# A 32-byte pad at the right edge of SBUF in an encoder-block kernel

## The chip, the cores and the metric

The kernel runs on one core of a Trainium2 chip. The metric is the device time of one execution in microseconds, as a median of runs; before the change it is 1386.01 us (three runs, 1385.64 to 1386.95).

## The reference

One encoder block with 1024 positions and a model width of 1024, all in float32. Cut to what matters:

```python
proj = x @ w_in[l]                      # q, k, v of attention; q, k, v, gates of the GLA; merge gates
...
y_attn = ...                            # three groups of dilated window attention, mixed
y_gla  = ...                            # gated linear attention in both directions, normed and gated
merged = (jax.nn.sigmoid(gate_a) * (y_attn @ w_attn_branch[l])
          + jax.nn.sigmoid(gate_g) * (y_gla @ w_gla_branch[l]))
x = _layernorm(ALPHA * x + merged @ w_out[l], ln1_g[l], ln1_b[l])
ff = jnp.square(jax.nn.relu(x @ w_ff1[l] + b_ff1[l])) @ w_ff2[l] + b_ff2[l]   # 1024 -> 4096 -> 1024
x = _layernorm(ALPHA * x + ff, ln2_g[l], ln2_b[l])
```

## The kernel before

**Products in three passes.** Each float32 operand is split into a high part that TensorE takes at full speed (float32r) and a low part, the rest; ScalarE writes the high one, VectorE the low one. The helper `mm3` then issues three matmuls for each slice of 128 of the sum, on its lines 101 to 103, so almost every matmul of the profile has one of these lines:

```python
for i, (lh, ll, rh, rl) in enumerate(pairs):
    T.matmul(ps, lh, rh, ...)           # line 101: stationary, moving
    T.matmul(ps, lh, rl, ...)           # line 102
    T.matmul(ps, ll, rh, ...)           # line 103
```

The first SBUF operand is stationary (128x128, loaded into the array ahead of the matmul; the profile shows the load as engine PEld), the second moves (128x512). In the profile both stand behind the arrow, as in `ps<-B,fwhi`.

**The stages, in order of time.** Input projections; attention and linear attention, woven together; then from about 597 us the branch stage (`merge_a`, `merge_g`), the output projection `wout`, the first layer norm (`ln1`, and transposes of its result in `x1t`), the first feed-forward product (`pair1`), the second (`group`), and the last layer norm (`fin`). A scheduler sets the order of instructions from the order of the code.

The two feed-forward products and most projections use Strassen-Winograd: seven products of half-size blocks instead of eight. Their operands are sides: tiles of the shape [128, 2, 4, 512] with the high and the low part. In the first product the activations are the moving sides B11, B21, B22, T1, T2, T3, T4, and the weights of a pair of column blocks are split into the stationary sides `fwhi`, `fwlo`, `fraw`, `wc`, two buffers deep ahead. A pair has seven steps of 12 matmuls, one for each of these moving sides; there are 16 pairs. Pairs 0 and 1 take two of their seven weight blocks from the tile `early`. In the second product 28 times (4 groups of 7) a left block (`hp`, the hidden layer read back from DRAM) and a right block (`wa`, `wb`, weights) are split into two of six tiles that are used in turn, in this order, two for a product of 48 matmuls:

```python
sides = [X[nm] for nm in ("B11", "B21", "T3", "T1", "T4", "B22")]
```

**The output projection.** `wout` runs over 8 row tiles for each half of the columns. Stationary is the merged activation `mg` (`mg00`, `mg01` for row tiles 0 to 3, `mg10`, `mg11` for 4 to 7), moving the weights, which for the first half are `wo`, for the second `whi` and `wlo`:

```python
merge_streams([lambda t=t, ks=ks: wout(t, 0, w, ps[t], ks) for ks in (range(0, 4), range(4, 8)) for t in range(8)],
              park(0) + park(1))
```

So the first half is four blocks of 48 matmuls: row tiles 0 to 3, 4 to 7, then both again.

**Where tiles lie.** A pool opens at the left end of SBUF's free space, or with `side="right"` at the right end, growing towards the left. The left pools start behind small constants at an address of 0 modulo 64 and hold tiles of multiples of 64 bytes where it matters here. The right end of what the pools may use is 229344, which is 32 modulo 64; so all big tiles of right pools lie at 32 modulo 64. From the branch stage on these are on the right: pool `actb` (line 1007: `mg00`, `mg01`, later `early`, `B22`, `T4`), `woa` and `wob` (`wo`), `c0`, `xraw`, `res` and `pf` (`hp`, `wa`). All else is on the left.

Of the kernel before, what the change touches and what calls it, by code (L numbers as in the profile page):

```python
# [7 lines left out]
F32 = mybir.dt.float32  # L8
# [63 lines left out]
def build(tc, io):  # L72
    nc = tc.nc
    V, G, A, T, SP = nc.vector, nc.gpsimd, nc.scalar, nc.tensor, nc.sync
    P = Pools(tc)
# [108 lines left out]
    for k in range(KT):  # L184
        n = {0: 1, 1: 1, 2: 2, 4: 2, 6: 2}.get(k)
# [759 lines left out]
    for i in range(8):  # L945

        n = n0 - 18 + i * 3 // 2
# [54 lines left out]
    def load_gate(wi, hf):  # L1002
        g = gtp.tile([128, 512], F32, tag="gate", bufs=9, name="gate")
        SP.dma_start(g, spill[wi, :, hf * 512:hf * 512 + 512])
        return g

    bp = P.open("actb", bufs=2, side="right")
    mg = [[bp.tile([128, 2, 4, 512], F32R, tag="actb", name=f"mg0{i}") for i in range(2)],
          [xp.tile([128, 2, 4, 512], F32R, tag="act", name=f"mg1{i}") for i in range(2)]]
# [149 lines left out]
    c0 = c0p.tile([128, 5, 512], F32, name="c0")  # L1159
# [308 lines left out]
    def run(steps, ahead):  # L1468
        for prep, _ in steps[:ahead]:
            prep()  # L1470
        for i, (_, do) in enumerate(steps):
            if i + ahead < len(steps):
                steps[i + ahead][0]()
            for f in do:
                f()
# [229 lines left out]
        (SP if t == 2 else A).dma_start(io["out"][t * 128:t * 128 + 128, lo:hi], h)  # L1705

    run([st for g in range(NG) for st in group(g)], 2)
    for n in ("r2", "acc2", "pf", "c0", "actb"):
        P.close(n)
    for n in ("ps8", "dram", "act", "const"):  # L1710
        P.close(n)
# [74 lines left out]
def make(arrays):  # L1786
    import concourse.bacc as _bacc
    nc = _bacc.Bacc("TRN2", target_bir_lowering=False, num_devices=1, dynamic_dma_scratch_size=1024)
    io = {}
    for n, a in arrays.items():  # L1790
        io[n] = nc.dram_tensor(f"in_{n}", a.shape, mybir.dt.from_np(a.dtype), kind="ExternalInput").ap()
    io["out"] = nc.dram_tensor("out_0", (S, D), F32, kind="ExternalOutput").ap()
    with tile.TileContext(nc, schedule_with_timeline_sim=True) as tc:
        build(tc, io)
    return nc
# [8 lines left out]
```

## Time and profile before

| | |
|---|---|
| timed runs | 1386.01 us median (1385.64 to 1386.95) |
| profiled execution | span 1382.5 us from the first to the last instruction; the page gives no other time for it |
| TensorE (PE) busy | 1373.9 us, 99% |
| weight loads (PEld) | 1152.6 us, 83%, beside the matmuls |
| VectorE (DVE) busy | 1010.4 us, 73% |
| ScalarE (ACT) busy | 630.6 us, 46% |
| GpSimd (POOL) busy | 99.3 us, 7% |
| HBM | 172 GB/s over the span |

How to read it: rows of the timeline give a start, a duration, engine, line, operation and tiles. A matmul's duration there (0.39 us) is that of a pipeline, and matmuls overlap; the rate is read from the starts of successive ones. Rows of windows give for a stretch its length, then for PE, PEld, DVE, ACT and POOL the busy time and the count of instructions, then TensorE's granted clock (1.00 is full), the share of the DMA engines that is busy, and GB/s. Rows of waits read "engine, what waited <- what ended the wait: us in total, times, longest".

### The profile page before, as it was taken

To read this page: it belongs to the slowest core of one execution; us is meant where nothing else is said; L and a number is where in the kernel's file an instruction comes from. 1 tells how busy PE (TensorE), PEld (TensorE's weight loads), DVE (VectorE), ACT (ScalarE), POOL (GpSimd) and SP (SyncE) were. 2 spreads that over 40 slices of the span, in tenths; PEclk is the share of its full clock that TensorE was granted. 3 is DMA by queue.
4 is the path that set the end of the run, shared out by engine and by line. 5 is a ranking of instruction groups with operands and counts; after the bars stand their busy time and mean duration, and the time that the engine had idled before them with its cause. 6 is when DMAs were issued, how large, how long until landed. Compare 5 with 4: busy or idle time off the path is not lost.

```text
span 1382.5 us, 19028 instructions
## 1 busy us (share of the span) xinstructions
PE 1373.9 (99%) x6837; PEld 1152.6 (83%) x6837; DVE 1010.4 (73%) x1748; ACT 630.6 (46%) x1207; POOL 99.3 (7%) x153
## 2 busy tenths in 40 slices
PE   9999999999999999999999999999999999999998
PEld 7989998888888888888888788888888888888886
DVE  6377768776665678567757777877767897786988
ACT  5356645334434344455316655555456433333333
POOL 0000100022322232000001000000000000000002
PEclk9999999999999999999999999999999999999999
DMA  7262326765554443465934465656654965445313
GB/s 256 62 204 74 120 72 219 205 198 156 172 163 136 133 148 125 153 226 190 342 121 177 168 233 191 215 204 213 224 200 150 373 210 167 152 130 161 105 31 122
DMA packets 105907, 238.57 MB, mean 173 GB/s; under 512 B 20101, under 2 KB 28805, under 8 KB 105812
## 3 DMA queue, kind: packets, MB, share of 16 engines
q1 hardware_dynamic: 99220, 218.47, 47.4%
q0 software_dynamic: 6304, 18.49, 4.4%
q8 instruction: 54, 0.88, 0.3%
q10 hardware_dynamic: 288, 0.39, 0.1%
q14 instruction: 41, 0.34, 0.1%
HBM read 160.67 MB, written 77.68 MB: 172 GB/s over the span
## 4 chain that ended last, share of the span: by engine, by line
PE 96%; DVE 2%; ACT 1%; issue 0%; DMA 0%; SPq 0%; ACTq 0%; DVEq 0%
PE ps L101 18%; PE ps L103 18%; PE ps L102 18%; PE mm L101 10%; PE mm L102 10%; PE mm L103 10%; PE avp L844 3%; PE sc L803 2%; PE tr L830 2%; PE ps L1192 0%; PE sc L406 0%; PE tr L376 0%; DVE L L341 0%; PE sc L101 0%; PE sc L103 0%; PE sc L102 0%
## 5 line engine op out<-in xcount | busy, mean ns | idle before, releaser
L1176 ACT CAST T<-hp 128x1024 fp32r<-128x1024 f32 x36 | 37.8, 1050 | 110.3 <-PE ps L102 70.6
L102 PE MATMUL mm<-wlo,x 128*128 128x272 f32 (+1 forms) x240 | 74.5, 310 | 0.7 <-DVE wlo L94 0.7
L101 PE MATMUL mm<-whi,x 128*128 128x272 f32 (+1 forms) x240 | 75.0, 313 | 0.0
L103 PE MATMUL mm<-whi,x 128*128 128x272 f32 (+1 forms) x240 | 74.7, 311 | 0.0
L814 ACT ACTIVATE e<-e,sm 128x256 f32<-128x256 f32 (+2 forms) x96 | 43.4, 453 | 51.7 <-DVE sm L809 51.7
L102 PE MATMUL ps<-B,B 128*128 128x512 f32 x160 | 62.4, 390 | 0.0
L103 PE MATMUL ps<-B,B 128*128 128x512 f32 x160 | 62.3, 389 | 0.0
L101 PE MATMUL ps<-B,B 128*128 128x512 f32 x160 | 61.0, 391 | 0.5 <-ACT B L1176 0.5
L103 PE MATMUL ps<-B,T 128*128 128x512 f32 x144 | 56.2, 390 | 0.0
L101 PE MATMUL ps<-B,T 128*128 128x512 f32 x144 | 56.2, 390 | 0.0
L103 PE MATMUL ps<-T,T 128*128 128x512 f32 x144 | 56.1, 390 | 0.0
L101 PE MATMUL ps<-T,T 128*128 128x512 f32 x144 | 56.0, 389 | 0.0
L102 PE MATMUL ps<-T,T 128*128 128x512 f32 x144 | 56.0, 389 | 0.0
L102 PE MATMUL ps<-B,T 128*128 128x512 f32 x144 | 56.0, 389 | 0.0
L1177 DVE TENSOR_TENSOR T<-hp,T 128x1024 fp32r<-128x1024 f32 x36 | 43.9, 1220 | 15.3 <-ACT T L1176 15.2
L1577 DVE TENSOR_TENSOR acc<-ps,acc 128x512 f32<-128x512 f32 x68 | 45.5, 684 | 12.9 <-PE ps L103 12.2
L642 DVE TENSOR_TENSOR cr<-cu,mm 128x512 f32<-128x512 f32 x44 | 35.1, 799 | 23.7 <-PE mm L103 23.5
L1682 POOL TENSOR_TENSOR mv<-mv,mhalf 128x1 f32<-128x1 f32 x8 | 7.1, 882 | 611.4 <-DVE mv L1681 609.9
L101 PE MATMUL mm<-x,pwlo 128*128 128x512 f32 x128 | 51.0, 398 | 0.0
L101 PE MATMUL ps<-T,fraw 128*128 128x512 f32 x128 | 50.0, 394 | 0.3 <-ACT T L1176 0.3
L102 PE MATMUL ps<-T,fraw 128*128 128x512 f32 x128 | 50.1, 392 | 0.0
L103 PE MATMUL ps<-T,fraw 128*128 128x512 f32 x128 | 50.1, 392 | 0.0
(497 smaller groups left out, 4227.3 us busy)
## 6 DMA issues: line engine op xcount, KB each, us to landing
hdr<-c SPq DMA_DIRECT2D x112, 256.0 KB, 2.3
hp<-hdr SPq DMA_DIRECT2D x56, 512.0 KB, 3.6
spill<-cr SPq DMA_DIRECT2D x64, 256.0 KB, 2.8
praw<-in_wfm SPq DMA_DIRECT2D x16, 512.0 KB, 5.0
pwhi<-in_wfm SPq DMA_DIRECT2D x16, 512.0 KB, 4.5
gate<-spill SPq DMA_DIRECT2D x32, 256.0 KB, 3.4
wa<-in_w SPq DMA_DIRECT2D x16, 512.0 KB, 4.7
wb<-in_w SPq DMA_DIRECT2D x16, 512.0 KB, 6.3
```

Source lines behind the costliest of these rows:

```text
L101: T.matmul(ps, lh, rh, start=first and i == 0, stop=False, skip_group_check=more)
L102: T.matmul(ps, lh, rl, start=False, stop=False, skip_group_check=more)
L103: issued["pe"] = T.matmul(ps, ll, rh, start=False, stop=last and i == n - 1, skip_group_check=more)
L642: issued["add"] = V.tensor_tensor(o, a, b, op=OP.add)
L803: mm = T.matmul(sps[i][:, pr, 0:w], q[ps_, pr], k[ps_, pr, 0:w], start=True, stop=True)
L814: issued["exp"] = A.activation(e, e, AF.Exp, bias=sm[:, h:h + 1], scale=-1.0, accum_out=sm[:, 4 + h:5 + h])
L830: T.transpose(tp[0:hi - lo, pr, j], b["e"][i][:, pr, lo:hi], ident)
L844: return T.matmul(av[:, h * 64:h * 64 + 64], b["et"][h % 2][p0:p0 + vv.shape[0], h // 2, j], vv[:, h * 64:h * 64 + 64], start=j == h == 0, ...
L1176: A.copy(o[:, 0], src)
L1177: V.tensor_tensor(o[:, 1], src, o[:, 0].bitcast(F32), op=OP.subtract)
L1577: V.tensor_tensor(m, p, m, op=OP.add)
L1682: G.tensor_tensor(mv[:, 3:4], mv[:, 2:3], mhalf[:, 0:1], op=OP.pow)
```

## The change

A pool `pad` with one tile of 8 float32 a partition, 32 bytes, is opened on the right ahead of the first right pool of the branch stage, and closed at the end. No instruction writes or reads it.

```diff
+    P.open("pad", side="right").tile([128, 8], F32, name="pad")
     bp = P.open("actb", bufs=2, side="right")
     mg = [[bp.tile([128, 2, 4, 512], F32R, tag="actb", name=f"mg0{i}") for i in range(2)],
           [xp.tile([128, 2, 4, 512], F32R, tag="act", name=f"mg1{i}") for i in range(2)]]
...
-    for n in ("r2", "acc2", "pf", "c0", "actb"):
+    for n in ("r2", "acc2", "pf", "c0", "actb", "pad"):
         P.close(n)
```

The addresses that the built programs give to the tiles (bytes within a partition; the rest modulo 64 in brackets):

| tiles | pool | before | after |
|---|---|---|---|
| mg00, early, T4 | actb, right | 196576 (32) | 196544 (0) |
| mg01, B22 | actb, right | 212960 (32) | 212928 (0) |
| wo, eight tiles | woa, wob, right | 163808 to 192480 (32) | 163776 to 192448 (0) |
| c0 | c0, right | 186336 (32) | 186304 (0) |
| xr0, xr1 | xraw, right | 153568, 169952 (32) | 153536, 169920 (0) |
| ga, bb, tb, four res | res, right | 165856 to 184288 (32) | 165824 to 184256 (0) |
| four hp, four wa | pf, right | 153568 to 182240 (32) | 153536 to 182208 (0) |
| mg10, T1 | act, left | 52160 (0) | the same |
| mg11, T3 | act, left | 19392 (0) | the same |
| B11, B21 | act, left | 3008, 35776 (0) | the same |
| T2 | x7, left | 112064 (0) | the same |
| fwhi, fwlo, fraw, whi, wlo | w, left | 68544 to 107712 (0) | the same |
| wc6 | f1, left | 132544 (0) | the same |
| px, x11 (input projections) | cx, act, left | 177600, 19392 (0) | the same |

In all, 31 tiles move by 32 bytes.

## The prediction

> **What bounds the kernel now.** I read the page from the top, then the waits of TensorE, then single stretches of the timeline. The page's head, its clock row and its chain:
>
> ```profile
> span 1382.5 us, 19028 instructions
> PE 1373.9 (99%) x6837; PEld 1152.6 (83%) x6837; DVE 1010.4 (73%) x1748; ACT 630.6 (46%) x1207; POOL 99.3 (7%) x153
> PEclk9999999999999999999999999999999999999999
> PE 96%; DVE 2%; ACT 1%; issue 0%; DMA 0%; SPq 0%; ACTq 0%; DVEq 0%
> ```
>
> The reader is to see that TensorE is busy 99% of the span, that 96% of the chain that ended last is TensorE, and that its clock is never throttled. What TensorE still waits for, in its four longest rows of the waits:
>
> ```profile
> PE zp L180 <- DVE mhalf L211: 1.2, 1, 1.2
> PE ps L1703 <- ACT dg L1702: 1.0, 1, 1.0
> PE mm L102 <- DVE wlo L94: 0.7, 2, 0.4
> PE mm L101 <- ACT x L148: 0.5, 1, 0.5
> ```
>
> That is 3.4 us of 1382.5, so no wait is worth removing; time can only come from the rate of the matmuls themselves. "A busy PE is not PE at its peak", so I looked at how fast equal matmuls follow each other. The output projection is made for this: four blocks of 48 matmuls of 128x512, alike but for where their operands lie. The stationary operand is mg, the moving one wo. Windows cut at the first matmul of each block, with the matmuls and weight loads on mg alone:
>
> ```profile
> core 0: us, PE busy (x) PEld busy (x) DVE busy (x) ACT busy (x), PEclk, DMA share, GB/s
> 661.59:672.50 10.91, 10.91 (x48) 9.01 (x48) 2.08 (x3) 1.79 (x3) 1.00 1.04 398
> 672.50:683.70 11.20, 11.20 (x50) 9.00 (x49) 0.00 (x0) 0.00 (x0) 1.00 0.79 263
> 683.70:694.58 10.88, 10.88 (x49) 9.01 (x48) 0.00 (x0) 0.00 (x0) 1.00 0.80 305
> 694.58:705.77 11.19, 11.19 (x49) 9.00 (x48) 0.00 (x0) 0.00 (x0) 1.00 0.46 180
> ```
>
> (Counts over 48 are neighbours that overlap the window's edge.) Blocks 1 and 3 read mg00 and mg01 from pools on the right, 2 and 4 read mg10 and mg11 from the pool act on the left; wo is on the right in all four. By the address table above, left tiles stand at 0 modulo 64 and right tiles at 32. So 1 and 3 pair 32 with 32: 10.91/48 = 227.3 ns and 10.88/48 = 226.7 ns a matmul. 2 and 4 pair 32 with 0: 11.20/48 = 233.3 and 11.19/48 = 233.1 ns. The DMA share falls through 1.04, 0.79, 0.80, 0.46 and does not follow the steps; the clock is 1.00 in all. The weight loads take 9.00/48 = 187.5 ns in fast and slow blocks alike: what slows is the stream of the moving operand, while the next weights are read beside it.
>
> Is it the address, or only that one tile is low in memory and the other high? The input projections have a pair that tells: stationary px at 177600, which is as high as wo, but in a left pool, and moving x at 19392. First matmul of a step of 12, and first of the next step:
>
> ```profile
> 245.74 0.39 PE L101 MATMUL mm<-x,px 128*128 128x512 f32 x1
> 248.46 0.39 PE L101 MATMUL mm<-x,pwlo 128*128 128x512 f32 x1
> ```
>
> 2.72 us for 12, which is 226.7 ns: far apart, both at 0 modulo 64, and fast. I take 226.7 ns as the rate without the conflict.
>
> **The change, part by part.** It adds no instruction and reorders none: each engine's instructions stand in the built program in the same order as before; only 31 tiles lie 32 bytes lower. All pairs that were 32 with 0 become 0 with 0, and 32 with 32 becomes 0 with 0 too. So the work is to count the matmuls that now pair 32 with 0, and to price one.
>
> They are 624. Output projection, first half (moving wo right, stationary mg10/mg11 left): 4 row tiles x 8 slices x 3 = 96. Second half (moving whi/wlo left, stationary mg00/mg01 right): 96. Early weights (stationary on the right, moving B11 and B21 on the left): 2 pairs x 2 steps x 12 = 48. First feed-forward product: in each of 16 pairs the steps with T4 and with B22 (moving right, stationary left), 32 x 12 = 384. In the second product the operands come from six sides, and the sides of the right pool, T4 and B22, are always used with each other: no mixed pair, except where a product of the one kind follows one of the other.
>
> The price in the first feed-forward product, step by step. The first row is T3 (left), the second and fourth T4 (right), the third and fifth B11 (left), all against left weights:
>
> ```profile
> 788.02:790.74 2.72, 2.72 (x13) 2.25 (x12) 2.49 (x4) 1.19 (x2) 0.00 (x0) 1.00 0.01 3
> 790.74:793.54 2.80, 2.80 (x13) 2.25 (x12) 2.76 (x5) 2.74 (x6) 0.00 (x0) 1.00 0.25 94
> 793.54:796.30 2.76, 2.76 (x13) 2.25 (x12) 2.76 (x6) 2.76 (x5) 0.00 (x0) 1.00 0.51 190
> 796.30:799.10 2.80, 2.80 (x13) 2.25 (x12) 2.80 (x6) 1.19 (x3) 0.00 (x0) 1.00 0.92 341
> 799.10:801.86 2.76, 2.76 (x13) 2.25 (x12) 2.76 (x6) 2.38 (x5) 0.00 (x0) 1.00 0.50 187
> ```
>
> A mixed step costs 0.08 us more than 2.72, and the clean step behind it still 0.04 more: the stream seems to need a few matmuls to settle. By these rows a mixed step is worth (11.12 - 4 x 2.72)/2 = 0.12 us. The longer stretches, which hold all such effects:
>
> ```profile
> 661.59:705.77 44.18, 44.18 (x193) 36.02 (x192) 31.06 (x43) 13.35 (x18) 0.00 (x0) 1.00 0.77 286
> 705.77:716.98 11.21, 11.21 (x50) 9.02 (x48) 4.45 (x8) 0.62 (x1) 0.57 (x1) 1.00 0.25 102
> 801.86:1060.17 258.31, 258.31 (x1130) 211.65 (x1128) 197.21 (x307) 136.60 (x218) 0.00 (x0) 1.00 0.60 203
> 1060.17:1076.68 16.51, 16.51 (x73) 13.51 (x72) 10.94 (x15) 10.83 (x16) 0.00 (x0) 1.00 0.71 222
> 1076.68:1131.19 54.51, 54.51 (x241) 45.04 (x240) 50.45 (x55) 22.78 (x24) 0.00 (x0) 1.00 0.90 327
> ```
>
> With the weight loads as the count of matmuls and 226.7 ns (2.72/12) as the floor:
> - Output projection, first half: 44.18 - 192 x 0.22667 = 0.66 us.
> - Second half: 11.21 - 48 x 0.22667 = 0.33 us for 48, twice: 0.66 us.
> - First feed-forward product: 258.31 - 1128 x 0.22667 = 2.63 us, which holds 26 of the 32 mixed steps (0.10 each); 16.51 - 72 x 0.22667 = 0.19 us for two more; 0.10 each for the four of the pairs 0 and 1: 3.22 us.
> - Second product: 54.51 - 240 x 0.22667 = 0.11 us. It has 28 products of 48, 27 of them behind 1076.68: 1296/240 x 0.11 = 0.59 us if all of it is due to the switches between kinds of pairs, about 0.2 if each of some 24 switches costs one matmul its 6.7 ns. I take the middle, 0.4.
> - Early weights: the rows below.
>
> ```profile
> 759.85 0.40 PE L102 MATMUL ps<-B,early 128*128 128x512 f32 x1
> 761.48 0.39 PE L103 MATMUL ps<-B,early 128*128 128x512 f32 x1
> 761.91 0.59 ACT c L1319
> 762.50 1.65 ACT T L1176 x4
> 764.68 2.80 ACT xr L1195 x8
> 768.62 1.24 PE ps L101 x4
> ```
>
> Seven matmuls in 1.63 us are 232.9 ns each, so 48 x 6.2 = 0.30 us. But from 761.91 to 768.62 the chain runs through ScalarE (the last four rows are of the chain), so the 24 matmuls beside it gain nothing: 0.15 us.
>
> Sum: 0.66 + 0.66 + 3.22 + 0.4 + 0.15 = 5.1 us, all on TensorE and nearly all on the chain. The weak term is the settling, since I know no cause for it. Without any of it, 624 less the 24 hidden matmuls by 6.2 ns give 3.7 us; with all of it 5.3.
>
> Other engines: I cost the 32 bytes at nothing there. VectorE's operations with two operands in SBUF, by where these lie (wb, T1 and T3 left; wa and hp right):
>
> ```profile
> L1554 DVE TENSOR_TENSOR wb<-wb,wb x8: 1212/1218/1222, 1087.1 to 1286.0; 128x1024 f32<-128x1024 f32 x8
> L1554 DVE TENSOR_TENSOR wb<-wb,wa x8: 1212/1216/1219, 1086.0 to 1284.3; 128x1024 f32<-128x1024 f32 x8
> L1554 DVE TENSOR_TENSOR wa<-wb,wa x8: 1214/1218/1220, 1083.7 to 1280.3; 128x1024 f32<-128x1024 f32 x8
> ```
>
> Medians of 1216 to 1218 ns for equal and for mixed addresses: no effect. If that cover fails, VectorE has room where it counts (197.21 of 258.31 us in the first feed-forward product).
>
> [...]
>
> **The rivals.**
> A, nothing changes. The slow pairs would then owe their 6 ns to something that goes with the sides, such as tag or distance, and keep it: 1386.0 us. Against it stands px, high and fast. For it: before has no left-right pair at equal addresses. [...]
> B, the gain in the first feed-forward product is taken back because ScalarE and VectorE can't prepare sides faster: 1386.0 - (5.1 - 3.2) = 1384.1 if all of it is. Against it: ScalarE waits there for TensorE to free its buffers,
>
> ```profile
> ACT fraw L1176 <- PE ps L102: 42.0, 23, 3.3
> ```
>
> so a faster TensorE frees them sooner. What would be late next is VectorE at 76%.
> C, slower: DMAs into the moved tiles land later. The page's issues:
>
> ```profile
> hp<-hdr SPq DMA_DIRECT2D x56, 512.0 KB, 3.6
> wa<-in_w SPq DMA_DIRECT2D x16, 512.0 KB, 4.7
> wb<-in_w SPq DMA_DIRECT2D x16, 512.0 KB, 6.3
> ```
>
> wa (right, 32) lands in 4.7 us and wb (left, 0), of the same size, in 6.3. If the address were the reason, wa at 0 would take 1.6 us more: 16 x 1.6 = 25.6 us of landing. It decides once over 5.1 us of that reaches TensorE, a fifth; with a half, 1386.0 - 5.1 + 12.8 = 1393.7. Against it: wb is issued right behind wa on the same queue, reason enough for 6.3, and the loads are issued two steps ahead, where a step of 48 lasts 10.9 us.
>
> **How the numbers follow.** The page gives no time for the profiled execution besides its span, 1382.5; the three timed runs have a median of 1386.01 (1385.64 to 1386.95), 3.5 above it. I take the gain off the median: 1386.0 - 5.1 = 1380.9 us, and 1377.4 for the span. Chances: the forecast 0.86, A 0.05, B 0.06, C 0.03. 0.2% (2.8 us, 1383.2) is about what a measurement of this kernel can tell from no change. The forecast and half of B lie beyond it: faster 0.89; A and the other half of B: same 0.08; C: slower 0.03. The range: gains of 3.7 to 5.3 us, 0.65 more on either side for how the runs before spread around 1386, and B's halfway house: 1379.9 to 1383.4.
>
> **What the profile after would show.** The windows of the output projection at 10.9 us for all four blocks, the five steps of the first feed-forward product at 2.72 each, and its 1128 matmuls in about 255.7 us instead of 258.3; weight loads still at 187.5 ns, VectorE's times unchanged. If blocks 2 and 4 keep 11.2, A is right; if they fall but the 1128 matmuls don't, B; if TensorE waits for hp or wa, C. If mixed steps fall to 2.72 and the steps behind them stay at 2.76, the settling was something else, and the gain is nearer 3.7.

## The result and the profile after

The changed kernel takes 1380.3 us (median of five runs, 1379.72 to 1383.76), where the one before takes 1386.0. The ratio of the times is 0.9961, with a 95% interval of 0.9949 to 0.9972: 5.4 us faster, 3.9 to 7.1 by the interval. The ratios here and below leave out two executions far off the rest, one of before at 2099.97 us and one of `both32` at 1515.93 us. The forecast was 1380.9.

The page of after, its head and its clock row:

```profile
span 1382.0 us, 19028 instructions
PE 1370.8 (99%) x6837; PEld 1153.0 (83%) x6837; DVE 1011.3 (73%) x1748; ACT 630.7 (46%) x1207; POOL 99.1 (7%) x153
PEclk9999999999999999999999999999999999999998
```

Its chain, and the three longest waits of TensorE:

```profile
PE 90%; DVE 3%; DMA 2%; issue 2%; ACT 2%; POOL 0%; SPq 0%; POOLq 0%; ACTq 0%; DVEq 0%
```

```profile
PE mm L101 <- DVE cu L642: 1.4, 1, 1.4
PE zp L180 <- DVE mhalf L211: 1.2, 1, 1.2
PE mm L101 <- ACT x L148: 1.0, 1, 1.0
```

TensorE still carries the chain and waits for little; that DMA stands in it with 2% is mostly due to loads in the input stage, such as `pwhi`, 5.08 us from 235.02 on. The instructions are as many as before, and TensorE is 3.1 us less busy in all. But the span is 1382.0 us, hardly below the 1382.5 of before, though the median fell by 5.7. The reader must look at where the stretch that the change touches begins and ends. The first matmul on `wo` and the last one of a product in three passes (below: the last matmul), in the timelines of before and of after:

```profile
661.59 0.39 PE L101 MATMUL ps<-wo,mg 128*128 128x512 f32 x1
1371.81 0.39 PE L103 MATMUL ps<-B,B 128*128 128x512 f32 x1
```

```profile
665.99 0.39 PE L101 MATMUL ps<-wo,mg 128*128 128x512 f32 x1
1370.81 0.39 PE L103 MATMUL ps<-B,B 128*128 128x512 f32 x1
```

From the one to the other it was 710.22 us and is now 704.82: 5.40 us less. Ahead of it, where no matmul reads a tile that has moved, this execution lost 4.40 us, all of it before the branch stage, whose first matmul on `ya` starts at 596.30 us in before and at 600.71 in after. Behind it 0.50 us were lost (10.69 us from the last of these matmuls to the end, now 11.19). It was the slowest timed run of after (1383.76 us); the other four have spans of 1377.9 to 1378.6. Such a difference in the start comes with any kernel here: the same first matmul on `wo` stands at 662.30, 662.62, 663.75 and 664.29 us in experiments below. So I compare kernels by their medians and by the distance between those two matmuls, which the start doesn't enter.

The four blocks of the output projection in after, by the same windows as before (matmuls and weight loads on `mg` alone; PE, PEld, DVE, ACT, clock, DMA share, GB/s):

```profile
665.99:676.87 10.88, 10.88 (x49) 9.01 (x48) 2.78 (x4) 2.46 (x4) 1.00 1.01 379
676.87:687.75 10.88, 10.88 (x50) 9.01 (x48) 0.00 (x0) 0.00 (x0) 1.00 0.75 281
687.75:698.63 10.88, 10.88 (x50) 9.01 (x48) 0.00 (x0) 0.00 (x0) 1.00 0.94 325
698.63:709.51 10.88, 10.88 (x50) 9.01 (x48) 0.00 (x0) 0.00 (x0) 1.00 0.41 157
```

All four last 10.88 us, which is 226.7 ns a matmul; the 11.20 and 11.19 of blocks 2 and 4 are gone, and the 10.91 of block 1 too. The weight loads took 9.00 to 9.01 us a block and take 9.01. The five steps of the first feed-forward product that stood at 2.72, 2.80, 2.76, 2.80 and 2.76 (these windows have POOL as well):

```profile
790.87:793.59 2.72, 2.72 (x13) 2.25 (x12) 2.49 (x4) 1.19 (x2) 0.00 (x0) 1.00 0.01 3
793.59:796.31 2.72, 2.72 (x13) 2.25 (x12) 2.68 (x5) 2.66 (x6) 0.00 (x0) 1.00 0.26 96
796.31:799.03 2.72, 2.72 (x13) 2.25 (x12) 2.72 (x5) 2.72 (x6) 0.00 (x0) 1.00 0.51 191
799.03:801.75 2.72, 2.72 (x13) 2.25 (x12) 2.72 (x6) 1.31 (x3) 0.00 (x0) 1.00 0.87 325
801.75:804.47 2.72, 2.72 (x13) 2.25 (x12) 2.72 (x5) 2.22 (x4) 0.00 (x0) 1.00 0.51 191
```

The mixed steps have lost their 0.08, and the clean steps behind them their 0.04. The longer stretches of after (second half of the output projection, its first 48 matmuls; from its last block to the third pair of the feed-forward product; then the stretches of the prediction):

```profile
709.51:720.39 10.88, 10.88 (x50) 9.01 (x48) 9.02 (x16) 1.86 (x3) 0.57 (x1) 1.00 0.48 195
758.29:804.47 46.18, 45.78 (x211) 37.63 (x210) 37.03 (x62) 32.36 (x68) 0.93 (x1) 1.00 0.55 207
804.47:1060.15 255.68, 255.68 (x1129) 211.72 (x1128) 197.63 (x308) 136.59 (x219) 0.00 (x0) 1.00 0.60 206
1060.15:1076.47 16.32, 16.32 (x73) 13.51 (x72) 10.87 (x15) 10.83 (x16) 0.00 (x0) 1.00 0.72 225
1076.47:1130.87 54.40, 54.40 (x241) 45.05 (x240) 50.33 (x55) 22.78 (x24) 0.00 (x0) 1.00 0.90 329
1349.27:1371.03 21.76, 21.76 (x97) 17.83 (x95) 20.81 (x51) 8.16 (x20) 4.58 (x5) 1.00 0.34 127
```

Two rows of before that the prediction doesn't show, the counterparts of the second and the last:

```profile
755.17:801.86 46.69, 46.42 (x211) 37.62 (x210) 37.27 (x63) 32.60 (x69) 0.93 (x1) 1.00 0.55 205
1350.02:1372.04 22.02, 22.02 (x97) 17.84 (x95) 20.84 (x51) 8.19 (x20) 4.59 (x5) 1.00 0.34 126
```

From these rows and from the ends of stretches in them, the whole of the 5.40 us is found again (the third row also holds two steps behind pairs 0 and 1):

| stretch | before | after | less | forecast |
|---|---|---|---|---|
| output projection, first half | 44.18 | 43.52 | 0.66 | 0.66 |
| second half, to the start of the next row | 49.40 | 48.78 | 0.62 | 0.66 |
| early weights, pairs 0 and 1 | 46.69 | 46.18 | 0.51 | 0.15 + 0.40 |
| 1128 matmuls of the first feed-forward product | 258.31 | 255.68 | 2.63 | 2.63 |
| its last 24, with the first 48 of the second product | 16.51 | 16.32 | 0.19 | 0.19 |
| the rest of the second product, to the last group's end piece | 273.34 | 272.80 | 0.54 | 0.4 in all |
| end piece, to the last matmul | 21.79 | 21.54 | 0.25 | |

VectorE's operations with two operands, the same three groups as before, which stood at 1218, 1216 and 1218 ns:

```profile
L1555 DVE TENSOR_TENSOR wb<-wb,wb x8: 1220/1224/1228, 1088.1 to 1285.4; 128x1024 f32<-128x1024 f32 x8
L1555 DVE TENSOR_TENSOR wb<-wb,wa x8: 1219/1221/1226, 1086.9 to 1283.7; 128x1024 f32<-128x1024 f32 x8
L1555 DVE TENSOR_TENSOR wa<-wb,wa x8: 1218/1220/1222, 1084.7 to 1279.7; 128x1024 f32<-128x1024 f32 x8
```

They are 2 to 6 ns longer, whether or not their operands changed their places against each other: nothing was won here, and nothing that matters lost.

### The profile page after: what moved, and what is told of

It is laid out like the page before. It is cut to its first block, busy times and chain, and to the rows that moved or that the text cites. A ratio compares the mean times of both kernels' runs of the same rounds, so it can differ in the third digit from the quotient of the medians.

```text
span 1382.0 us, 19028 instructions
## 1 busy us (share of the span) xinstructions
PE 1370.8 (99%) x6837; PEld 1153.0 (83%) x6837; DVE 1011.3 (73%) x1748; ACT 630.7 (46%) x1207; POOL 99.1 (7%) x153
## 4 chain that ended last, share of the span: by engine, by line
PE 90%; DVE 3%; DMA 2%; issue 2%; ACT 2%; POOL 0%; SPq 0%; POOLq 0%; ACTq 0%; DVEq 0%
PE ps L101 18%; PE ps L102 18%; PE ps L103 18%; PE mm L101 9%; PE mm L102 9%; PE mm L103 9%; PE avp L844 2%; PE tr L830 1%; PE sc L803 1%; ACT xr L1196 1%; DMA xrh<-in_xT 1%; DMA praw<-in_wfm 1%; PE sc L406 0%; PE tr L376 0%; DMA pwhi<-in_wfm 0%
## 5 line engine op out<-in xcount | busy, mean ns | idle before, releaser
L1178 DVE TENSOR_TENSOR T<-hp,T 128x1024 fp32r<-128x1024 f32 x36 | 44.1, 1224 | 14.1 <-ACT T L1177 14.0
L101 PE MATMUL mm<-x,pwlo 128*128 128x512 f32 x128 | 51.1, 399 | 1.4 <-DVE cu L642 1.4
L103 PE MATMUL mm<-x,pwlo 128*128 128x512 f32 x128 | 50.0, 391 | 0.0
L102 PE MATMUL mm<-x,pwlo 128*128 128x512 f32 x128 | 50.0, 391 | 0.0
L101 PE MATMUL ps<-T,fraw 128*128 128x512 f32 x128 | 49.6, 390 | 0.4 <-ACT T L1177 0.4
```

The costliest lines, as they stand in the source:

```text
L101: T.matmul(ps, lh, rh, start=first and i == 0, stop=False, skip_group_check=more)
L102: T.matmul(ps, lh, rl, start=False, stop=False, skip_group_check=more)
L103: issued["pe"] = T.matmul(ps, ll, rh, start=False, stop=last and i == n - 1, skip_group_check=more)
L1178: V.tensor_tensor(o[:, 1], src, o[:, 0].bitcast(F32), op=OP.subtract)
```

## The experiments

The theory of the prediction (1): a matmul is slowed when its moving operand and the weights loaded beside it, those of the next matmul, differ in their address modulo 64. Its rivals: (2) the operand must start at a multiple of 64; (3) what counts is the side, left or right, or the distance; (4) the pad brings something else. Later a fifth came up: (5) as 1, but modulo 256.

**All at 32 instead of all at 0.** From the kernel before, a pad of 32 bytes on the left, ahead of everything, and none on the right. All big tiles then stand at 32 modulo 64. (To make room, two small tiles became one; nothing is computed otherwise.)

```diff
+    cp.tile([128, 8], F32, name="padl")
...
-    ... ring(ap_, [128, 5, 4], F32, 2, "f")
+    ... (lambda f2: turns([f2[:, i] for i in range(2)], 2))(ap_.tile([128, 2, 5, 4], F32, name="f"))
```

> The kernel before, with 32 bytes put at the left edge in place of the right one, so that left and right tiles all stand at 32 modulo 64. Theory 1 (what counts is whether the moving operand and the weights read beside it differ modulo 64): no pair differs any more, so the same gain as the change, 1380 to 1381 us, all four blocks of the output projection 10.9 us. Theory 2 (what counts is that an operand starts at a multiple of 64): nothing stands at one now, so no gain, 1386 us or more, and the blocks take 11.2 us. Theory 3 (left against right, or distance, whatever the address): 1386 us, blocks as before, 10.9 and 11.2 in turn.

1380.55 us (1379.45 to 1381.78), before 1386.15, ratio 0.9957 (0.9944 to 0.9971): the whole gain, and 704.82 us between the two matmuls, as in after. The first two blocks of the output projection:

```profile
663.21:674.09 10.88, 10.88 (x49) 9.01 (x49) 2.08 (x3) 1.87 (x3) 1.00 1.01 401
674.09:684.97 10.88, 10.88 (x50) 9.02 (x49) 0.00 (x0) 0.00 (x0) 1.00 0.75 258
```

No big tile starts at a multiple of 64 here, every tile is on its side as before, and there is no pad on the right: theory 2 falls, of theory 3 the side, and of theory 4 anything that only a pad on the right could bring. The distance between left and right tiles is 32 bytes less than before, as in after; that it isn't the distance as such is shown by the pad of 288 bytes further down.

**Both pads.** From after, the left pad too, with the two small tiles again as one: right tiles at 0, left tiles at 32 modulo 64.

```diff
+    cp.tile([128, 8], F32, name="padl")
...
     P.open("pad", side="right").tile([128, 8], F32, name="pad")
```

> The change and 32 bytes at the left edge besides: right tiles at 0, left ones at 32 modulo 64. Theory 1 (difference): the 624 mixed pairs are back, 1386 us, blocks of the output projection 10.9 and 11.2 us in turn. Theory 2 (multiples of 64): the pairs with both tiles on the right are at 0 and fast, those on the left are not: between 1381 and well over 1386 us, since most pairs are on the left. Theory 3 (left against right): 1386 us here too, but then the change itself should have gained nothing.

1386.51 us, ratio 1.0001 (0.9992 to 1.001): the gain is gone. Blocks 1 and 2:

```profile
664.29:675.20 10.91, 10.91 (x49) 9.02 (x48) 2.48 (x4) 1.87 (x3) 1.00 1.01 404
675.20:686.39 11.19, 11.19 (x49) 9.02 (x48) 0.00 (x0) 0.00 (x0) 1.00 0.82 264
```

So the pad on the right is worth nothing by itself; what counts is the difference between the addresses of the two sides. The settling (10.91) is back with it.

**A pad of 64 bytes.** The pad moves all right tiles as far again, but leaves them at 32 modulo 64.

```diff
-    P.open("pad", side="right").tile([128, 8], F32, name="pad")
+    P.open("pad", side="right").tile([128, 16], F32, name="pad")
```

> The pad doubled to 64 bytes: right tiles move by 64 and stay at 32 modulo 64. Theory 1 and theory 2: no gain, 1386.0 us within 0.1%, mixed blocks 11.2 us. Theory 4 (the gain comes from another thing that a pad brings, such as a gap at the edge or a moved DMA target, not from the address modulo 64): a gain as with 32 bytes, 1380 to 1381 us.

1386.13 us, ratio 1.0 (0.9991 to 1.0009), and the blocks as before:

```profile
662.30:673.22 10.92, 10.92 (x49) 9.02 (x49) 2.77 (x4) 2.47 (x4) 1.00 1.01 386
673.22:684.43 11.21, 11.21 (x50) 9.03 (x49) 0.00 (x0) 0.00 (x0) 1.00 0.79 278
```

So a pad as such did nothing here: 1386.13 us against 1386.15 before beside it.

**Other differences, tile by tile.** Four variants of the changed kernel, with the tiles of pool `actb` shifted inside wider buffers, each by bytes of its own, to find from which difference on the price is due.

```diff
+    AT = dict(mg00=16, mg01=48, early=16, B22=16, T4=48)      # offs_a; offs_b: 4, 8, 4, 4, 8; offs_c: 64, 128, 64, 64, 128
+                                                              # offs_d: 192, 32, 192, 192, 32
+    def bt(name, shape=(2, 4, 512)):
+        t = bp.tile([128, 4128], F32R, tag="actb", name=name)[:, AT[name] // 4:AT[name] // 4 + 4096]
         ...
```

> The change, with the tiles of the pool actb set off by 16 bytes (mg00, early, T4: no, mg00, early, B22 and T4 get 16 and 48 as follows: mg00, early, B22 and T4 stand in buffers that start at 0 modulo 64, with mg00 and early and B22 and T4 at 16 or 48: mg00 16, mg01 48, early 16, B22 16, T4 48). Which differences cost? If every difference that isn't a multiple of 64 costs: blocks 1 and 3 of the output projection (wo at 0 against 16 and 48) 11.2 us, blocks 2 and 4 (0 against 0) 10.9, steps with B22 and T4 2.80 us, and in the second product T4 with B22 (32 apart) 11.2 us for 48. If only the bit worth 32 counts: 16 costs nothing (10.9), 48 costs (11.2). If less than 32 is free on both sides of a line and the cost grows with the difference: 16 and 48 about half, 11.05. If 0 isn't the best difference, one of them is below 10.88 us.

> The change, with tiles of the pool actb set off by 4 bytes (mg00, early, B22) and 8 bytes (mg01, T4). Theory 1 as it stands (any difference modulo 64 costs): steps of the first feed-forward product with B22 and T4 2.80 us, early weights 233 ns, T4 with B22 (4 apart) 11.2 us for 48. A line of 16 bytes or more as the reason (small differences share a line): 2.72, 226.7 ns and 10.9. If equal addresses are not the best case: under 2.72 us for one of them.

> The change, with tiles of the pool actb set off by 64 bytes (mg00, early, B22) and 128 bytes (mg01, T4). Theory 1 (modulo 64): nothing costs, all steps of 12 at 2.72 us, all blocks of 48 at 10.9. If the period is 128 or more: the tiles set off by 64 cost as much as 32 did, 2.80 us for B22 and 11.2 us for the blocks with mg00, and T4 with B22 (64 apart) 11.2; with a period of 256 those set off by 128 too.

> The change, with mg00, early and B22 set off by 192 bytes and mg01 and T4 by 32, in buffers that both start at the left tiles' address modulo 256. Theory 5: all of it costs: blocks 1 and 3 of the output projection 11.2 us, steps with B22 and T4 2.80 us, T4 with B22 (160 apart) 11.2 us for 48; blocks 2 and 4 10.9. The part with 32 bytes (block 3, T4) also says whether the kernels with set-off tiles show what the kernel before shows for 32. If the cost depends on distance or sign, 192 (that is -64) differs from 32.

One flaw of mine: in the first three the wider buffer has 16512 bytes, 64 x 258, so that the second buffer of the pool (`mg01`, `B22`) stands another 128 off modulo 256, which modulo 64 cannot be seen. In offs_d (16640 bytes) it doesn't. One execution of each took 1389.03, 1392.61, 1388.39 and 1388.97 us (before beside them 1386.15, 1386.85, 1386.85 and 1386.22, where 1386.85 is a single execution too): all slower than before, in part because `B22` and `T4`, which are used with each other, now differ too (a product of 48 with them takes 11.20 us in offs_a, 11.50 in offs_b, 11.01 in offs_c); theory 1 has the multiples of 64 (offs_c) as fast as after. The blocks of the output projection in offs_c:

```profile
664.25:675.45 11.20, 11.20 (x49) 9.05 (x48) 2.66 (x4) 1.86 (x3) 1.00 1.01 397
675.45:686.36 10.91, 10.91 (x50) 9.02 (x48) 0.00 (x0) 0.00 (x0) 1.00 0.82 269
686.36:697.24 10.88, 10.88 (x50) 9.01 (x48) 0.00 (x0) 0.00 (x0) 1.00 0.94 359
697.24:708.12 10.88, 10.88 (x50) 9.02 (x48) 0.00 (x0) 0.00 (x0) 1.00 0.31 123
```

Block 1 pairs `wo` with `mg00`, which is 64 bytes further: equal modulo 64, and still 11.20 us. Block 3 pairs it with `mg01`, shifted by 128 and by the other 128 of its buffer, 256 together: 10.88. That was the first sign that the price goes modulo 256 and not 64. The prices differ too. In offs_d `mg00` stands 192 further, in offs_a `mg01` 48 + 128; and in offs_b a product of the second feed-forward product with both its sides from `actb` is slowed. In this order:

```profile
663.81:674.79 10.98, 10.98 (x48) 9.01 (x48) 2.08 (x3) 1.85 (x3) 1.00 1.01 396
```

```profile
684.98:696.01 11.03, 11.03 (x49) 9.00 (x48) 0.00 (x0) 0.00 (x0) 1.00 0.90 338
```

```profile
1258.14:1269.64 11.50, 11.50 (x50) 9.24 (x49) 7.32 (x9) 4.00 (x5) 0.00 (x0) 1.00 0.30 91
```

10.98 us is 228.8 ns a matmul, 11.03 is 229.8, 11.50 is 239.6. Windows from the first 512-wide matmul of a block, a step or a product to the first of the next one give, by the address of the moving operand less that of the next weights, modulo 256:

| difference | ns a matmul | seen in |
|---|---|---|
| 0 | 226.7 | 10.88 us for 48: all four blocks of after, left32 and right288 |
| 8 | 233.3 | 2.80 us for 12: `T4` in offs_b |
| 32 | 233.1 to 233.3 | 11.20 and 11.19 for 48: blocks 2 and 4 of before; 2.80 for 12: `T4` in before and offs_d |
| 48 | 234.2 | 2.81 for 12: `T4` in offs_a |
| 64 | 228.8, 229.4 | 10.98 for 48: block 1 of offs_d; 11.01: `B22` with `T4` in offs_c |
| 80 | 229.8 | 11.03: block 3 of offs_a |
| 96 | 233.3 | 11.20: `B22` with `T4` in offs_a |
| 120 | 233.1 | 11.19: block 3 of offs_b |
| 124 | 239.6 | 11.50: `B22` with `T4` in offs_b |
| 128 | 232.5 | 11.16: blocks 2 and 4 of right160 |
| 192 | 233.1 to 233.3 | 11.20: block 1 of offs_c; 11.20 and 11.19: blocks 2 and 4 of right96 |
| 224 | 233.1 to 233.5 | 11.19 to 11.21: blocks 2 and 4 of both32 and right64, block 3 of offs_d |
| 252 | 232.5 | 11.16: block 1 of offs_b |
| 240 | 226.7; 232.0 and 233.5 in two other places | 10.88: block 1 of offs_a; the others by the starts of its matmuls |

None of these differences is cheaper than 0, and 64 costs a third to two fifths of what most others cost (2.1 and 2.7 ns, where most cost about 6.6). The last row has an exception that I can't explain, a single block of one execution: `wo` against `mg00` at 16 bytes' distance takes 226.7 ns, while `whi` and `wlo`, at the same address modulo 256 as `wo`, do not.

The input projections of before set a bound to this. There the moving slices of `whi` and `wlo` have 272 float32, 1088 bytes, so that from slice to slice they move on by 64 modulo 256 against the weights `x`, which stay where they are. The first of three matmuls of each slice, with differences of 0, 64, 128 and 192, and then 0 again:

```profile
34.78 0.29 PE L101 MATMUL mm<-whi,x 128*128 128x272 f32 x1
35.16 0.29 PE L101 MATMUL mm<-whi,x 128*128 128x272 f32 x1
35.53 0.29 PE L101 MATMUL mm<-whi,x 128*128 128x272 f32 x1
35.92 0.29 PE L101 MATMUL mm<-whi,x 128*128 128x272 f32 x1
36.29 0.29 PE L101 MATMUL mm<-whi,x 128*128 128x272 f32 x1
```

Three matmuls take 0.38, 0.37, 0.39 and 0.37 us. At this width the three at 64 and at 192 take no longer than those at 0 (0.37 us against 0.38), and those at 128 0.01 us longer: the price is shown for 512-wide matmuls alone.

**Whose address: the own weights or the next?** In all of the above a matmul's own weights and the next ones are mostly of one tile. In the last group of the second product stand two products one after the other, one with both sides on the right, one with both on the left. Woven matmul by matmul, each has its own operands equal and the next weights on the other side. `inter` does this to the kernel before, `inter_pad` to after.

```diff
-                prod1("Z", *sd[3], True, early(0, 1), tt)
-                prod1("X", *sd[2], True, late(0, 0), tt)
+                for k in range(4):
+                    for p in range(3):
+                        for b in "ZX":
+                            l, r = sd[3 if b == "Z" else 2]
+                            ... T.matmul(ps[b][tt], l[:, p // 2, k, ts], r[:, p % 2, k], ...)
```

> The kernel before, with the last two products of the last group woven matmul by matmul in place of twelve by twelve: B22 with T4 (32 with 32) in turn with B21 and B11 (0 with 0). In no matmul the own operands differ, but each runs while weights at the other address are loaded for the next. If it is the next weights that count: all 96 are slow, 233 to 235 ns, 24 in 5.6 us (before: 12 and 12 in 5.51). If a matmul's own weights count: 226.7 ns, 24 in 5.44 us.

> The same weaving with the pad, so that all addresses agree modulo 64: by theory 1 226.7 ns a matmul, 24 in 5.44 us. If the weaving itself costs something, such as the switch of output banks, it shows here.

The timeline of `inter`, the first of the woven matmuls and the 88th:

```profile
1351.73 0.39 PE L1645 MATMUL ps<-B,T 128*128 128x512 f32 x1
1371.91 0.39 PE L1645 MATMUL ps<-B,B 128*128 128x512 f32 x1
```

20.18 us for 87, 232.0 ns each. And of `inter_pad`:

```profile
1346.95 0.39 PE L1646 MATMUL ps<-B,T 128*128 128x512 f32 x1
1366.67 0.39 PE L1646 MATMUL ps<-B,B 128*128 128x512 f32 x1
```

19.72 us for 87, 226.7 ns. Weaving costs nothing where all addresses agree, and equal own operands don't help where the next weights differ. By this the price falls due between a matmul and the weights that are loaded while it runs (in the timeline of before the load for a matmul of line 102 starts at 672.51 us, 0.01 behind the matmul of line 101 ahead of it, which starts at 672.50). One rival is left: in `inter` successive moving operands also come from different sides, and no run has that without different next weights. I had expected slightly more than the 232.0.

**Modulo 64, 128 or 256?** The pad alone, in three more sizes:

```diff
-    P.open("pad", side="right").tile([128, 8], F32, name="pad")
+    P.open("pad", side="right").tile([128, 24], F32, name="pad")      # right96; right160: 40; right288: 72
```

> A pad of 96 bytes: right tiles agree with left ones modulo 64, but differ by 64 modulo 128 and 256. Theory 1 (modulo 64): the gain of the change, 1380 to 1381 us, all blocks of the output projection 10.9 us. Theory 5 (after the runs with set-off tiles, where 64 and 128 cost too: only addresses that agree modulo 256 are fast): no gain, 1386 us, mixed blocks 11.2 us.

> A pad of 160 bytes: left and right differ by 128 modulo 256. Theory 1 (modulo 64) and a period of 128: 1380 to 1381 us. Theory 5 (modulo 256): 1386 us, mixed blocks about 11.2 us.

> A pad of 288 bytes: left and right agree modulo 256, but right tiles stand 256 lower than with the 32-byte pad, so that some pairs differ by 256 modulo 512. Theory 1 and theory 5: the gain of the change, 1380 to 1381 us. If the period is 512 or the gain of the change came from anything but addresses modulo 256: slower than that, up to 1386 us.

With 96 bytes the sides agree modulo 64 and not 128; with 160 modulo 128 and not 256; with 288 modulo 256 and not 512. Left tiles all stand at 192 modulo 256; right tiles at 224 before, at 192 after the pad of 32.

| pad | medians (before beside it) | ratio, interval | first wo to last matmul |
|---|---|---|---|
| 96 | 1385.76 (1386.22) | 0.9993 (0.9984 to 1.0001) | 709.29 |
| 160 | 1385.09 (1386.22) | 0.9992 (0.9983 to 1.0001) | 708.97 |
| 288 | 1380.41 (1386.22) | 0.9958 (0.9945 to 0.997) | 704.81 |

Block 2 of each, in this order:

```profile
674.64:685.84 11.20, 11.20 (x50) 9.02 (x48) 0.00 (x0) 0.00 (x0) 1.00 0.76 263
```

```profile
673.35:684.51 11.16, 11.16 (x50) 9.04 (x48) 0.00 (x0) 0.00 (x0) 1.00 0.75 255
```

```profile
673.50:684.38 10.88, 10.88 (x49) 9.01 (x48) 0.00 (x0) 0.00 (x0) 1.00 0.77 268
```

In these runs agreement modulo 64 or 128 brings next to nothing (11.20 and 11.16 us for block 2), agreement modulo 256 brings all (10.88), and more than 256 isn't needed. For the 512-wide matmuls shown theory 5 stands, but for the exception at 240, and theory 1 was it with too small a number. No kernel beats after; left32 and right288 equal it.

## Why the prediction was right, and where it wasn't

- **What bounds the kernel.** Right: TensorE's rate, read from the starts of equal matmuls. The distance between the two marked matmuls fell by 5.40 us, where the sum had 5.1. The full speed of float32r stands in the traces as those 226.7 ns a matmul of 128x512 at a granted clock of 1.00; the four records of the plain float32 products of that width in the last layer norm (`acc,dg`, from 1374.47 us on in before) take 1.98 us.
- **Output projection, early weights, first feed-forward product.** Forecast 0.66 + 0.66 + 0.15 + 3.22, measured 0.66 + 0.62 and 0.51 + 2.63 + 0.19 (the third stretch holds the early weights and the pairs 0 and 1 together). The 226.7 ns taken from the pair `px` and `x` is what the matmuls of all blocks and steps shown of after take.
- **Second product: mis-sized.** Forecast 0.4, bounds 0.2 to 0.59; measured 0.54 + 0.25 = 0.79. I took the middle; the upper bound's rate, 0.11 us for 240 matmuls, held up to the end piece: it has 1200 matmuls ahead of it, which gives 0.55. The end piece I counted at the same rate, 0.04. Its two products take turns every 12 matmuls, eight stretches instead of two of 48, and it gave 0.25, about 0.03 for each stretch.
- **The settling.** Called the weak term, without a cause. It came and went with the mixing: where all agree all blocks shown stand at 10.88 (after, left32, right288), none at 10.91, and of the five steps shown of after none at 2.76; with both pads 10.91 comes back. What makes a few matmuls behind a switch slow was not found.
- **"Modulo 64": the step that failed.** The count of 624 and the prices were right by luck: 32 bytes happen to make the sides agree modulo 256 as well (224 to 192). By the rule as I put it, pads of 96 and 160 bytes, both of which bring the right tiles to 0 modulo 64, would have won as much; they took 0.9 and 1.3 us off the distance between the marked matmuls (709.29 and 708.97, from 710.22), not 5.4. What held, as far as `inter` shows it, is that the price hangs on the moving operand and the weights loaded beside it.
- **Rival A** (nothing changes) fell with left32, which leaves every tile on its side and has all four blocks at 10.88 us. Between inter and inter_pad, too, only addresses differ, and a matmul takes 232.0 or 226.7 ns.
- **Rival B** (ScalarE or VectorE late next) didn't come: the 1128 matmuls gained the full 2.63 us, with VectorE at 197.63 of 255.68. **Rival C** (DMAs into the moved tiles land later) neither: `wa`, now at 0 modulo 64, lands in 4.5 us by the page of after, where it took 4.7, and the second product got shorter.
- **The span** was forecast at 1377.4 and is 1382.0 in the profiled execution, because that run lost 4.40 us ahead of the first matmul that the change touches and 0.50 behind the last. The median, 1380.3, is where it was expected.
- **The range.** Its lower end, 1379.9, doesn't follow from its own terms: 1386.0 - 5.3 - 0.65 is 1380.05. The measured time lies above both.

What stays open: why the price goes by the addresses modulo 256 in these runs, and why it differs so between differences; the exception at 16 bytes; and why the 272-wide matmuls shown are spared. No trace shows a cause.

## What to carry to other kernels

Where TensorE is busy nearly all of the span with 512-wide matmuls and loads new weights for each, place the moving tiles and the weight tiles so that a moving operand and the weights loaded beside it agree modulo 256: here that took a block of 48 from 11.20 to 10.88 us. The pad costs no instruction (19028 before and after). Look for it by the starts of successive equal matmuls in blocks that differ only in the tiles they read, at the width in question, since the busy share says 99% of both kernels here. And test an address rule with more than one size of pad, since one size that works fits several rules.

## What the hardware showed that I had not expected

- In these runs a float32r matmul of 128x512 with its next weights loaded beside it took 226.7 ns where the two agree modulo 256, and otherwise mostly 232 to 234, from 228.8 (64 bytes apart) to 239.6 (124 apart), with one pair at 226.7 though 240 apart. Three 272-wide ones took 0.37 to 0.39 us, whether the two are 0, 64, 128 or 192 apart. The weight loads' own time does not tell: 9.01 us for 48 in a block of 10.88 (after), 9.02 in one of 11.20 (right96).
- Agreement modulo 64 or 128 was not enough: pairs that agree modulo 64 alone took 11.20 us for 48 (right96), modulo 128 alone 11.16 (right160), where 10.88 is to be had.
- VectorE's operations with two operands, of the three groups shown, had no such effect: 1216 to 1224 ns whichever way they lay.
